# A hybrid encoder step on one core: sums for the feed-forward made beside the output projections, and norm roots with tokens on partitions

## The chip, the cores and the metric

The kernel runs on one core of a Trainium2 chip. The core has five engines that run side by side, each through its own list of instructions in order: TensorE (PE, matmuls; PEld is its load of weights), VectorE (DVE), ScalarE (ACT), GpSimd (POOL) and SyncE (SP, which issues transfers). They wait for each other through semaphores. The metric is the device time of one execution, in microseconds, as the median of several runs.

## What is computed

One inference step of a two-layer encoder over 1072 tokens (32 of a sample, 16 meta tokens and 1024 of a prompt), 1024 features, in fp32. Every layer is

```python
x += mixer(rms_norm(x)) @ w_out          # layer 0: gated delta rule and S5; layer 1: two kinds of attention
h = rms_norm(x)
x += (silu(h @ w1) * (h @ w3)) @ w2      # feed-forward, 2816 wide
```

and a last `rms_norm` follows, with `rms_norm(x) = x * rsqrt(mean(x*x) + 1e-6) * gain`. The states and caches that the mixers leave are outputs too.

## The kernel before

Features lie on partitions and tokens on columns, so x is eight tiles `X[0..7]` of 128 features by 1072 tokens. The columns are cut in three chunks (360, 360, 352). To keep fp32 accuracy, every operand is split in a high part (ACT, L37 or L40) and a low part (DVE, L38 or L41), and each product is three matmuls (`mm3`, L72 to L74).

**The feed-forward** multiplies by w1 and w3 with a scheme of seven products for each 2 by 2 block (`quad`, Strassen-Winograd). The columns are halved (HN = 536) and the features too, so that `X[i]` and `X[i + 4]` form a pair, i = 0..3, with the blocks B11 and B12 (first and second half of the columns of `X[i]`) and B21 and B22 (of `X[i + 4]`). Seven right operands come from them: B11, B21, B22, and the sums T1 to T4, each for four pairs: 28 units, each a tile with its high and low part. T1 is the second half less the first of `X[i]`; T2, T3 and T4 need both tiles of a pair (`s_early`, L170 to L173, three scalar-tensor-tensors on DVE with the gain multiplied in). `s_late` makes the other sixteen, with the subtractions of T1 on POOL (L188). The weights have sums of their own, S1 to S4, on POOL (L206 to L209). The products run in the order B11, T2, B21, T3, T1, T4, B22, each as 24 matmuls of 268 columns (`pq`, L225); the first leaves its PSUM bank by ACT (L230). Eleven steps of `ffn` each take two row blocks of w1 and w3. The result goes through DRAM to the product with w2.

**The seam** is what lies between a layer's output projection and these products. The units are tiles of pools that `open_ffn` opens: 16 slots `mv`, 3 `ot`, 9 `us`, and scratch `sab`. It is called when the projections' own tiles (the mixers' output split in high and low part: `lh`, `ll`, `rh`, `rl` in layer 0, `mxh`, `mxl` in layer 1) are given back, so that no unit has a place before.

In layer 0, `out_part` adds the projection tile by tile to X (L1248): m = 5, 6, 7 with all twelve mixes, then 0 to 4 with the last eight. In layer 1 the loop over `ORD` (5, 6, 7, 0 to 4) adds the product of the heads 0 to 6 (L1473); the share of the eighth, `m7`, follows in a pass of 72 matmuls over all tiles (L1487).

**The norm** is not applied ahead of the products: its root `r` is multiplied into their results. `sq_acc` sums the squares of X over the tiles (ACT L94, POOL L95); `norm_r` sums over the partitions with a matmul by a matrix of ones (L83), so that every partition has the sum of each column, and takes Sqrt (L84) and the reciprocal (L85) of 128 by 360 values.

The order on each engine is set by a scheduler that weighs each instruction by estimated times; a tile that a pool reuses makes its first writer wait for the last reader of what lay there.

Of the kernel before, what the change touches and what calls it, by code (L numbers as in the profile page):

```python
# [11 lines left out]
T = 1072  # L12
# [3 lines left out]
SQ = 448  # L16
# [60 lines left out]
def norm_r(cx, acc, r, c0, c1, n=D, ps=None):  # L77

    nc = cx.nc
    p = (cx.ps.tile([128, 512], F32, name="pm", bufs=cx.npm) if ps is None else ps)[:, :c1 - c0]  # L80
    accs = acc if isinstance(acc, list) else [acc]
    for i, a in enumerate(accs):
        nc.tensor.matmul(p, cx.ones, a[:, c0:c1], start=i == 0, stop=i == len(accs) - 1)  # L83
    nc.scalar.activation(r[:, c0:c1], p, AF.Sqrt, bias=cx.eps, scale=1.0 / n)  # L84
    nc.vector.reciprocal(r[:, c0:c1], r[:, c0:c1])  # L85


def sq_acc(cx, x, acc, k, c0, c1, eng=None):
# [4 lines left out]
    s = cx.tp.tile([128, SQ], F32, name="sq", bufs=2)[:, :c1 - c0]  # L93
# [27 lines left out]
def open_ffn(cx, m7=None):  # L121

    cx.fA, cx.fB = ExitStack(), ExitStack()
    pa = cx.fA.enter_context(tpool(cx.tc, "fa"))
    pb = cx.fB.enter_context(tpool(cx.tc, "fb"))
    cx.tp = cx.fB.enter_context(tpool(cx.tc, "ftmp", 2))
    n = [0, 0]

    def slot(nm, bufs, dt=F32):
        return pa.tile([128, T], dt, name=nm, bufs=bufs)  # L130

    def us():
# [30 lines left out]
def s_early(cx, B, gain, i):  # L163
# [8 lines left out]
    v.scalar_tensor_tensor(b[:, n1], x1[:, n0], g1, b[:, n0], op0=OP.mult, op1=OP.add)  # L172
    v.scalar_tensor_tensor(a[:, n1], x2[:, n0], g2, b[:, n1], op0=OP.mult, op1=OP.subtract)  # L173
    for nm, src in (("T2", b[:, n1]), ("T3", b[:, n0]), ("T4", a[:, n1])):
        B[nm][i] = cx.us()
        s_parts(cx, src, B[nm][i])


def s_late(cx, B, gain):
    nc = cx.nc  # L180
    n0, n1 = slice(0, HN), slice(HN, T)
    for nm, h, n in (("B11", 0, n0), ("B21", 4, n0), ("T1", 0, None), ("B22", 4, n1)):
        for i in PAIRS:
            B[nm][i] = cx.slot("mv", 16, F32R)
            x, g = cx.X[i + h], gain[:, i + h:i + h + 1]
            if n is None:
                d = cx.sab()[:, n0]
                nc.gpsimd.tensor_sub(d, x[:, n1], x[:, n0])  # L188
                s_parts(cx, d, B[nm][i], scale=g)
            else:  # L190
                s_parts(cx, x[:, n], B[nm][i], scale=g)
# [6 lines left out]
def quad(cx, raws, B, first):  # L198
# [7 lines left out]
    g.tensor_add(S1, A21, A22)  # L206
    g.tensor_sub(S2, S1, A11)
    g.tensor_sub(S3, A11, A21)
    g.tensor_sub(S4, A12, S2)  # L209
# [38 lines left out]
def ffn(cx, w1, w3, w2, B, chunks, done, out=None):  # L248
# [3 lines left out]
    r = cx.slot("r", 1)  # L252
# [7 lines left out]
    with tpool(cx.tc, "sps", space=PSUM) as cx.ps:  # L260
        for t in range(0, 22, 2):
# [12 lines left out]
            o1, o2 = quad(cx, wa, B, gate)  # L274
# [5 lines left out]
            u1, u2 = quad(cx, wb, B, lambda o, p: v.tensor_mul(two(o), p, two(o1[:, :HN])))  # L280
# [70 lines left out]
def setup2(cx, tc, ctx, I):  # L351
# [395 lines left out]
def even_layer(cx, ctx, I, O):  # L747
# [13 lines left out]
    with ExitStack() as es:  # L761
# [1287 lines left out]
```

## Time and profile before

| | |
|---|---|
| median of 3 runs | 3412.39 us (3411.39 to 3413.61) |
| the profiled execution | 3411.61 us, of which the span is 3409.8 |
| PE busy | 3169.7 us, 93% |
| DVE, ACT, POOL busy | 58%, 35%, 32% |
| mean granted clock of PE | 0.964 |

The span is the stretch from the first to the last instruction of the trace. Busy times are sums over the whole span, while the seams are short; so they are read from stretches and from the rows of one engine in time. In such a row the first number is the start, the second the duration (of all, where a count stands behind), and brackets give the idle time of the engine ahead of it and what ended it.

### The profile page before, as it was taken

What the parts mean: (1) busy time and instruction counts of PE and PEld (TensorE: products, weight loads), DVE (VectorE), ACT (ScalarE), POOL (GpSimd) and SP (SyncE); (2) the same over time, 40 slices, a digit from 0 to 9 for tenths busy, and PEclk for the clock granted to TensorE, in tenths of its full rate; (3) what the DMA queues carried; (4) which work ended last, traced back from release to release, by engine and by line L of the source; (5) the groups of instructions that cost most, each with busy time, mean ns of one, the idle gap of its engine ahead of it and who ended that gap; (6) DMA issues with size and microseconds to landing.
All of it is one profiled execution on the core that took longest, in us unless ns stands there. A gap on an engine that the chain in (4) does not pass through costs nothing.

```text
span 3409.8 us, 54300 instructions
## 1 busy us (share of the span) xinstructions
PE 3169.7 (93%) x21511; PEld 3028.3 (89%) x21511; DVE 1961.1 (58%) x3590; ACT 1198.4 (35%) x2201; POOL 1092.5 (32%) x1080
## 2 busy tenths in 40 slices
PE   7998999999996999999999999998897899999997
PEld 6998998888895999999999998876687899999996
DVE  8666448945426555556338226657767655556435
ACT  5543222145523222223114115555653322223112
POOL 2144564512223555541003002223213655551003
PEclk9999999999998999999999999998898899999998
DMA  2355323356431222226123445544333222226212
GB/s 102 129 172 162 112 84 111 93 178 258 162 119 57 77 82 76 76 83 221 55 58 124 156 139 139 157 140 118 91 124 117 69 76 76 82 76 222 76 41 70
DMA packets 159525, 388.53 MB, mean 114 GB/s; under 512 B 40908, under 2 KB 72032, under 8 KB 159272
## 3 DMA queue, kind: packets, MB, share of 16 engines
q1 hardware_dynamic: 135096, 317.84, 29.8%
q10 hardware_dynamic: 16704, 44.33, 3.5%
q0 software_dynamic: 7472, 22.91, 2.0%
q8 instruction: 169, 2.77, 0.3%
q14 instruction: 84, 0.69, 0.1%
HBM read 265.44 MB, written 119.56 MB: 113 GB/s over the span
## 4 chain that ended last, share of the span: by engine, by line
PE 66%; DVE 5%; DMA 3%; ACT 2%; issue 2%; POOL 1%; SPq 0%; ACTq 0%; DVEq 0%; POOLq 0%
PE pq L225 26%; PE pm L72 10%; PE pm L73 10%; PE pm L74 10%; PE po L1765 1%; PE S L1583 1%; PE S L1580 1%; DVE mv L41 1%; PE tr L1760 1%; PE po L1847 1%; DMA sab<-ud 0%; PE pm L1695 0%; DMA rraw<-mixd 0%; POOL aQ L1568 0%; ACT P L1792 0%
## 5 line engine op out<-in xcount | busy, mean ns | idle before, releaser
L72 PE MATMUL pm<-mv,wh 128*128 128x360 f32 (+2 forms) x2080 | 692.2, 333 | 23.6 <-DVE pre L914 12.5
L73 PE MATMUL pm<-mv,wh 128*128 128x360 f32 (+2 forms) x2080 | 687.9, 331 | 0.0
L74 PE MATMUL pm<-mv,wl 128*128 128x360 f32 (+2 forms) x2080 | 685.4, 330 | 0.0
L72 PEld LDWEIGHTS pm<-mv,wh 128*128 128x128 f32 (+1 forms) x2080 | 393.5, 189 | 35.0 <-issue 12.8
L73 PEld LDWEIGHTS pm<-mv,wh 128*128 128x128 f32 (+1 forms) x2080 | 393.3, 189 | 4.4 <-issue 1.3
L37 ACT ACTIVATE wh<-wraw 128x1024 fp32r<-128x1024 f32 (+6 forms) x180 | 148.4, 824 | 706.5 <-PE pm L73 607.9
L74 PEld LDWEIGHTS pm<-mv,wl 128*128 128x128 f32 (+1 forms) x2080 | 393.5, 189 | 3.1 <-issue 0.2
L225 PE MATMUL pq<-mv,wl 128*128 128x268 f32 x2112 | 290.1, 293 | 36.4 <-ACT xslot L230 27.2
L225 PEld LDWEIGHTS pq<-mv,wl 128*128 128x128 f32 x2112 | 278.0, 195 | 39.9 <-ACT xslot L230 28.8
L95 POOL TENSOR_TENSOR acc<-acc,sq 128x360 f32<-128x360 f32 (+3 forms) x77 | 84.6, 1106 | 668.9 <-ACT sq L94 668.2
L225 PE MATMUL pq<-mv,wh 128*128 128x268 f32 x2112 | 279.1, 286 | 2.0 <-ACT wh L37 1.4
L225 PEld LDWEIGHTS pq<-mv,wh 128*128 128x128 f32 x2112 | 267.8, 188 | 2.6 <-ACT wh L37 1.9
L225 PE MATMUL pq<-us,wh 128*128 128x268 f32 x1188 | 163.6, 288 | 15.4 <-ACT wh L37 14.2
L312 DVE TENSOR_TENSOR xslot<-xslot,pm 128x360 f32<-128x360 f32 x144 | 75.2, 526 | 175.5 <-PE pm L74 175.4
L225 PEld LDWEIGHTS pq<-us,wh 128*128 128x128 f32 x1188 | 154.2, 190 | 16.3 <-ACT wh L37 16.3
L38 DVE TENSOR_TENSOR wl<-wraw,wh 128x1024 fp32r<-128x1024 f32 (+6 forms) x142 | 134.6, 948 | 53.1 <-ACT wh L37 51.6
L225 PE MATMUL pq<-us,wl 128*128 128x268 f32 x1188 | 162.3, 288 | 0.0
L225 PEld LDWEIGHTS pq<-us,wl 128*128 128x128 f32 x1188 | 153.6, 190 | 0.0
L279 POOL TENSOR_TENSOR xslot<-xslot,r 128x1072 f32<-128x1072 f32 x44 | 122.4, 2804 | 0.2
L921 DVE SCALAR_TENSOR_TENSOR cy<-pre,convw,cy 128x1104 f32<-128x1104 f32 x72 | 112.1, 1557 | 13.6 <-ACT cy L919 12.1
L38 DVE TENSOR_TENSOR wh<-sab,wh 128x512 fp32r<-128x512 f32 x88 | 78.7, 896 | 64.9 <-ACT wh L37 64.9
L1580 PE MATMUL S<-aKh,aQ 128*128 128x512 f32 (+9 forms) x240 | 91.8, 384 | 18.7 <-DVE mxs L1791 6.9
(718 smaller groups left out, 7152.8 us busy)
## 6 DMA issues: line engine op xcount, KB each, us to landing
ud<-xslot SPq DMA_DIRECT2D x44, 536.0 KB
sab<-ud SPq DMA_DIRECT2D x44, 536.0 KB
wraw<-in_w_dram SPq DMA_DIRECT2D x44, 512.0 KB
xraw<-in_w_dram SPq DMA_DIRECT2D x44, 512.0 KB
wraw<-in_wie_dram SPq DMA_DIRECT2D x36, 512.0 KB
qkvd<-cy ACTq DMA_DIRECT2D x24, 552.0 KB
wraw<-in_wio_dram SPq DMA_DIRECT2D x24, 512.0 KB
kq<-qkvd SPq DMA_DIRECT2D x16, 552.0 KB
```

The lines of the kernel that those rows point to most:

```text
L37: nc.scalar.activation(h, src, AF.Copy)
L38: (eng or nc.vector).tensor_sub(l, src, f(h))
L41: nc.vector.scalar_tensor_tensor(l, src, scale, f(h), op0=OP.mult, op1=OP.subtract)
L72: nc.tensor.matmul(ps, a, h[:, c0:c1], start=start and k == 0, stop=False)
L73: nc.tensor.matmul(ps, a, l[:, c0:c1], start=False, stop=False)
L74: nc.tensor.matmul(ps, b, h[:, c0:c1], start=False, stop=stop and k == kt - 1)
L95: (eng or nc.gpsimd).tensor_add(acc[:, c0:c1], acc[:, c0:c1], s)
L225: nc.tensor.matmul(p[:, 512 * j:512 * j + HC], op[:, wo + 128 * k:wo + 128 * k + 128], B[nm][k][:, xo + HC * j:xo + HC * j + HC], start=ne ...
L279: g.tensor_mul(o, o, r)
L312: nc.vector.tensor_add(X[m][:, c0:c1], X[m][:, c0:c1], p)
L921: v.scalar_tensor_tensor(y[:, :TG], pre[:, j:j + TG], convw[:, i, j:j + 1], y[:, :TG], op0=OP.mult, op1=OP.add)
L1580: nc.tensor.matmul(pt, lhs, Kh[:, k0:k0 + n], start=True, stop=False)
```

## The change

Five things change.

- **Pools.** `open_fa` (slots `mv`, `ot`, `r`) is opened ahead of the last part of the output projection. In layer 0 the late mixes now lie in `mv` slots themselves, with `ot` as landing place. `open_fb` (`us`, `sab`) follows, and a table `UNITS` says for every unit which kind of slot it takes, and in which order. In layer 0 the units of pairs 1 and 2 take `us`, which lies over `rh` and `rl`, and most others `mv`. In layer 1 they lie over the first four mixes, and in the tiles of `m7` and of the mixes 4 to 6 (`u7`, `u8`).
- **Order of tiles.** In layer 0 `m = 5` and `6` are projected together, first with the old mixes, then with the late ones. In layer 1 the order is 5, 6, 7, 1, 2, 3, 0, 4, and `m7` is the eighth head of the loop; the pass behind it is gone.
- **Engines.** The additions of squares beside the projections, the subtractions of T1, and S1 to S4 of the first step (`t == 0`) go from POOL to DVE.
- **Order of sums.** `s_all` makes T2 to T4 of pairs 1 and 2, B11, then pairs 3 and 0, then B21, T1 and B22. `s_early` splits T2 as soon as it is there.
- **Norm.** `norm_r` multiplies the slices of 128 tokens by one column of ones, so that the sums have tokens on partitions. Sqrt and reciprocal work on up to three columns; a second matmul per slice, by the identity, spreads them over the partitions again, and ACT copies the result to `r`. This holds for the norms at the start of both layers and at the end, too.

```diff
 def norm_r(cx, acc, r, c0, c1, n=D, ps=None):
-    for i, a in enumerate(accs):
-        nc.tensor.matmul(p, cx.ones, a[:, c0:c1], start=i == 0, stop=i == len(accs) - 1)
-    nc.scalar.activation(r[:, c0:c1], p, AF.Sqrt, bias=cx.eps, scale=1.0 / n)
-    nc.vector.reciprocal(r[:, c0:c1], r[:, c0:c1])
+    cuts = [(i, c, min(c + 128, c1)) for i, c in enumerate(range(c0, c1, 128))]
+    q = p[:, 508:512]
+    for i, a, b in cuts:
+        for j, x in enumerate(accs):
+            nc.tensor.matmul(q[:b - a, i:i + 1], x[:, a:b], cx.ones[:, 0:1], start=j == 0, stop=j == len(accs) - 1)
+    s = r[:, c0:c0 + 4]
+    for x0, x1, m in ((0, len(cuts) - 1, 128), (len(cuts) - 1, len(cuts), cuts[-1][2] - cuts[-1][1])):
+        nc.scalar.activation(s[:m, x0:x1], q[:m, x0:x1], AF.Sqrt, bias=cx.eps[:m], scale=1.0 / n)
+        nc.vector.reciprocal(s[:m, x0:x1], s[:m, x0:x1])
+    for i, a, b in cuts:
+        nc.tensor.matmul(p[:, a - c0:b - c0], s[:b - a, i:i + 1].to_broadcast([b - a, 128]), cx.ident[:b - a, :b - a], start=True, stop=True)
+    nc.scalar.activation(r[:, c0:c1], p[:, :c1 - c0], AF.Copy)
...
+UNITS = (
+    [("us", n, i) for i in (1, 2) for n in ("T2", "T3", "T4")] + [("us", "B11", i) for i in (1, 2, 3)] +
+    [("ot", "B11", 0), ("ot", "T2", 3), ("ot", "T3", 3), ("mv", "T4", 3)] + [("mv", n, 0) for n in ("T2", "T3", "T4")] +
+    [("mv", n, i) for n in ("B21", "T1", "B22") for i in PAIRS],
...
+def s_block(cx, B, gain, nm):
...
-                nc.gpsimd.tensor_sub(d, x[:, n1], x[:, n0])
+            cx.nc.vector.tensor_sub(d, x[:, n1], x[:, n0])
...
+def s_all(cx, B, gain):
+    s_early(cx, B, gain, 1)
+    s_early(cx, B, gain, 2)
+    s_block(cx, B, gain, "B11")
+    s_early(cx, B, gain, 3)
+    s_early(cx, B, gain, 0)
+    for nm in ("B21", "T1", "B22"):
+        s_block(cx, B, gain, nm)
...
-            o1, o2 = quad(cx, wa, B, gate)
+            o1, o2 = quad(cx, wa, B, gate, g if t else v)
...
+    with esX:
+        open_fa(cx)
         open_psum(cx, False)
-        mv += [load_mix(k, sp, "l", 7) for k in range(1, 8)]
-        out_part(range(5, 8), [(mvs, 0), (mv, 4)], cx.pmt, True)
-        out_part(range(5), [(mv, 4)], cx.pmt, True)
+        mv = [load_mix(k, ltiles) for k in range(8)]
+        out_part([5, 6], [(mvs, 0), (mv, 4)], cx.pmt, True)
+        out_part([7], [(mvs, 0), (mv, 4)], cx.pmt, True)
+        for m in range(5):
+            out_part([m], [(mv, 4)], cx.pmt, True)
...
-ORD = list(range(NF, 8)) + list(range(NF))
+ORD = [5, 6, 7, 1, 2, 3, 0, 4]
...
-        mix += [parts(k, mp) for k in range(4, 7)]
+        mix += [parts(k, lambda n: more["u8"]()) for k in range(4, 7)] + [m7]
...
-                mm3(cx, p, w, mix[k0:], 7 - k0, 128, c0, c1)
+                mm3(cx, p, w, mix[k0:], 8 - k0, 128, c0, c1)
                 v.tensor_add(x[:, c0:c1], x[:, c0:c1], p)
+                sq_acc(cx, x, cx.acc, i, c0, c1, v)
```

How the change moves instructions shows in the order on the engines. First DVE in layer 0, around the last evictions of the projection (L1248 before, L1279 after); `xslot` and `xraw` are tiles of X. Before, the evictions stand alone and all sums follow:

```order
L1248 TENSOR_TENSOR xslot<-xslot,pm 128x360 x2
L1248 TENSOR_TENSOR xslot<-xslot,pm 128x352
L38 TENSOR_TENSOR wl<-wraw,wl 128x512
L1248 TENSOR_TENSOR xslot<-xslot,pm 128x360 x2
L1248 TENSOR_TENSOR xslot<-xslot,pm 128x352
L41 SCALAR_TENSOR_TENSOR mv<-xraw,gain,mv 128x536
L41 SCALAR_TENSOR_TENSOR mv<-xslot,gain,mv 128x536 x3
```

After, in the same place, with the sums of pair 3 (L192 to L195) and their splits among the evictions of the last tile:

```order
L192 SCALAR_TENSOR_TENSOR sab<-xslot,gain,sab 128x536
L193 SCALAR_TENSOR_TENSOR sab<-xslot,gain,sab 128x536
L195 SCALAR_TENSOR_TENSOR sab<-xslot,gain,sab 128x536
L1279 TENSOR_TENSOR xslot<-xslot,pm 128x360
L38 TENSOR_TENSOR ot<-sab,ot 128x536 x2
L104 TENSOR_TENSOR acc<-acc,sq 128x360
L1279 TENSOR_TENSOR xslot<-xslot,pm 128x360
L38 TENSOR_TENSOR mv<-sab,mv 128x536
L104 TENSOR_TENSOR acc<-acc,sq 128x360
L1279 TENSOR_TENSOR xslot<-xslot,pm 128x352
L192 SCALAR_TENSOR_TENSOR sab<-xslot,gain,sab 128x536
L208 TENSOR_TENSOR sab<-xraw 128x536
```

Three of four pairs, and B11, have moved ahead of the last eviction; pair 0, T1 (L208), B21 and B22 still follow it.

Next PE at the start of layer 1's feed-forward. Before, the end of the pass for `m7` (its tiles are called `sab`), B11, the norm, B21 and the first matmuls of T2:

```order
L74 MATMUL pm<-sab,wl 128x352
L225 MATMUL pq<-mv,wl 128x268 x24
L83 MATMUL pm<-acc,ones 128x360 x2
L83 MATMUL pm<-acc,ones 128x352
L225 MATMUL pq<-mv,wl 128x268 x24
L225 MATMUL pq<-us,wh 128x268 x4
```

After, where the last projection matmul is one of the loop:

```order
L74 MATMUL tr<-u_22125,wl 128x352
L255 MATMUL pq<-mv,wl 128x268 x24
L87 MATMUL pm<-ones,acc 128x1 x2
L87 MATMUL pm<-ones,acc 104x1
L87 MATMUL pm<-ones,acc 128x1 x2
L87 MATMUL pm<-ones,acc 104x1
L93 MATMUL pm<-ident,r 128x128 x2
L93 MATMUL pm<-ident,r 128x104
L93 MATMUL pm<-ident,r 128x128 x2
L93 MATMUL pm<-ident,r 128x104
L255 MATMUL pq<-mv,wl 128x268 x2
```

Each norm has become two visits to PE, one column per slice (L87) and a spreading matmul (L93), which here stand directly behind each other, between B11 and B21.

## Rows read from the trace of the kernel before

**Rows 1.** The page: busy us of each engine, share of the span, instructions
```profile
PE 3169.7 (93%) x21511; PEld 3028.3 (89%) x21511; DVE 1961.1 (58%) x3590; ACT 1198.4 (35%) x2201; POOL 1092.5 (32%) x1080
```

**Rows 2.** What PE waited for: us in all, times, longest
```profile
PE pq L225 <- ACT xslot L230: 27.2, 2, 24.5
...
PE pm L83 <- POOL acc L95: 19.4, 3, 11.3
```

**Rows 3.** Layer 0's seam: length, busy us of PE, PEld, DVE, ACT, POOL, granted clock
```profile
1040.00:1060.00 20.00, 19.90 (x120) 19.35 (x119) 3.48 (x8) 4.05 (x8) 4.79 (x5) 1.00 0.11 41
1060.00:1080.00 20.00, 4.94 (x28) 3.38 (x27) 20.00 (x24) 12.05 (x21) 1.59 (x1) 0.79 0.07 28
1080.00:1105.00 25.00, 7.50 (x35) 6.97 (x36) 22.32 (x24) 12.62 (x20) 17.86 (x10) 0.57 0.20 63
1105.00:1150.00 45.00, 43.38 (x334) 42.99 (x334) 28.63 (x30) 13.12 (x19) 24.57 (x15) 0.95 0.21 72
```

**Rows 4.** PE there, in time: start, us, instruction, count, idle before with releaser
```profile
1058.73 0.32 PE L74 MATMUL pm<-lh,wl 128*128 128x352 f32 x1
...
1062.76 2.97 PE L225 MATMUL pq<-mv,wl 128*128 128x268 f32 x22 [0.47 <-DVE mv L41]
...
1092.26 4.63 PE L225 MATMUL pq<-mv,wl 128*128 128x268 f32 x24 [24.51 <-ACT xslot L230]
...
1104.29 4.83 PE L225 MATMUL pq<-mv,wl 128*128 128x268 f32 x20 [1.83 <-DVE wl L38]
```

**Rows 5.** DVE in the same stretch
```profile
1059.09 0.52 DVE L1248 TENSOR_TENSOR xslot<-xslot,pm 128x352 f32<-128x352 f32 x1 [3.34 <-PE pm L74]
...
1060.56 2.15 DVE L41 SCALAR_TENSOR_TENSOR mv<-xslot,gain,mv 128x536 fp32r<-128x536 f32 x3
...
1065.97 4.66 DVE L85 RECIPROCAL r<-r 128x360 f32<-128x360 f32 x2
...
1078.63 1.97 DVE L38 TENSOR_TENSOR us<-sab,us 128x536 fp32r<-128x536 f32 x3
...
1098.39 4.17 DVE L41 SCALAR_TENSOR_TENSOR mv<-xslot,gain,mv 128x536 fp32r<-128x536 f32 x3
```

**Rows 6.** POOL in the same stretch
```profile
1094.40 1.79 POOL L206 TENSOR_TENSOR sab<-wraw 128x512 f32<-128x512 f32 x1
```

**Rows 7.** Stretches of layer 1's seam, columns as in rows 3
```profile
2580.00:2600.00 20.00, 20.00 (x125) 20.00 (x124) 9.93 (x18) 2.64 (x4) 0.00 (x0) 1.00 0.26 77
2620.00:2640.00 20.00, 6.25 (x16) 3.08 (x15) 19.96 (x21) 11.34 (x22) 12.18 (x10) 0.59 0.00 0
2640.00:2665.00 25.00, 10.08 (x42) 9.46 (x43) 25.00 (x22) 10.36 (x17) 15.16 (x10) 0.57 0.21 64
```

**Rows 8.** PE in layer 1's seam, columns as in rows 4
```profile
2612.20 0.32 PE L74 MATMUL pm<-sab,wl 128*128 128x352 f32 x1
...
2662.80 3.72 PE L225 MATMUL pq<-mv,wl 128*128 128x268 f32 x15 [1.45 <-DVE wl L38]
```

**Rows 9.** DVE there: additions that read PSUM
```profile
2601.92 2.27 DVE L1487 TENSOR_TENSOR xraw<-xraw,pm 128x360 f32<-128x360 f32 x5
```

**Rows 10.** PE in time: the first matmul with a late mix
```profile
957.97 0.65 PE L72 MATMUL pm<-lh,wh 128*128 128x360 f32 x3
```

**Rows 11.** ACT in time: the last two splits of late mixes
```profile
968.01 1.10 ACT L37 ACTIVATE lh<-lraw 128x1072 fp32r<-128x1072 f32 x1 [1.30 <-DMA lraw<-mixd]
972.45 1.10 ACT L37 ACTIVATE lh<-lraw 128x1072 fp32r<-128x1072 f32 x1 [3.33 <-DMA lraw<-mixd]
```

**Rows 12.** A stretch of layer 0's start, columns as in rows 3
```profile
30.00:40.00 10.00, 7.73 (x35) 5.77 (x34) 10.00 (x23) 4.90 (x6) 3.11 (x4) 0.86 0.01 2
```

**Rows 13.** DVE in time at the end
```profile
3383.33 2.45 DVE L85 RECIPROCAL mv<-mv 128x368 f32<-128x368 f32 x1 [6.47 <-ACT mv L84]
...
3395.63 1.75 DVE L85 RECIPROCAL mv<-mv 128x256 f32<-128x256 f32 x1 [1.82 <-ACT mv L84]
```

**Rows 14.** PE in time at the end
```profile
3393.86 1.22 PE L83 MATMUL pm<-acc,ones 128*128 128x256 f32 x2 [3.43 <-DVE acc L95]
```

More of the change, by code (lines that the diff above doesn't have):

```diff
@@ L92, in sq_acc @@
         return
-    s = cx.tp.tile([128, SQ], F32, name="sq", bufs=2)[:, :c1 - c0]
+    s = cx.sqt()[:, :c1 - c0]
     nc.scalar.activation(s, x[:, c0:c1], AF.Square)
@@ L172, in s_early, with quad @@
     v.scalar_tensor_tensor(b[:, n1], x1[:, n0], g1, b[:, n0], op0=OP.mult, op1=OP.add)
+    s_parts(cx, b[:, n1], B["T2"][i])
     v.scalar_tensor_tensor(a[:, n1], x2[:, n0], g2, b[:, n1], op0=OP.mult, op1=OP.subtract)
[L174 to L180, printed above, removed]
-    n0, n1 = slice(0, HN), slice(HN, T)
[L182 to L187, printed above, removed]
-                nc.gpsimd.tensor_sub(d, x[:, n1], x[:, n0])
-                s_parts(cx, d, B[nm][i], scale=g)
-            else:
-                s_parts(cx, x[:, n], B[nm][i], scale=g)
+    s_parts(cx, b[:, n0], B["T3"][i])
+    s_parts(cx, a[:, n1], B["T4"][i])
+def s_block(cx, B, gain, nm):
+    n0, n1 = slice(0, HN), slice(HN, T)
+    h, n = {"B11": (0, n0), "B21": (4, n0), "T1": (0, None), "B22": (4, n1)}[nm]
+    for i in PAIRS:
+        x, g = cx.X[i + h], gain[:, i + h:i + h + 1]
+        if n is None:
+            d = cx.sab()[:, n0]
+            cx.nc.vector.tensor_sub(d, x[:, n1], x[:, n0])
+            s_parts(cx, d, B[nm][i], scale=g)
+        else:
+            s_parts(cx, x[:, n], B[nm][i], scale=g)
+def s_all(cx, B, gain):
[6 more added lines that the diff above has]
+        s_block(cx, B, gain, nm)
 def two(ap):
     return ap.rearrange("p (b n) -> p b n", b=2)
-def quad(cx, raws, B, first):
+def quad(cx, raws, B, first, eng):
     nc = cx.nc
@@ L1427, in odd_layer @@
     m7 = esM.enter_context(tpool(tc, "m7"))
-    m7p, m7 = m7, [m7.tile([128, T], F32R, name="sab", bufs=2) for e in range(2)]
+    m7p, m7 = m7, [m7.tile([128, T], F32R, name="u7", bufs=2) for e in range(2)]
     def out_w(m, k0, k1):
@@ L1437, in odd_layer, with parts @@
             at.diff(m7, 3)
-        def parts(k, pool):
+        def parts(k, slots):
             raw = hi.tile([128, T], F32, name="oraw", bufs=2)
@@ L1446, in parts @@
                 g.tensor_mul(raw[:, 32:], raw[:, 32:], w)
-            h, l = (pool.tile([128, T], F32R, name=n, bufs=4) for n in ("mxh", "mxl"))
+            h, l = (slots(n) for n in "hl")
             split(cx, raw, h, l)
             return h, l
-        mix = [parts(k, hi) for k in range(4)]
+        mix = [parts(k, lambda n: hi.tile([128, T], F32R, name="mx" + n, bufs=4)) for k in range(4)]
         for m in range(NF):
@@ L1459, in odd_layer @@
             g.dma_start(xd2[m], x)
+        m8 = esM.enter_context(tpool(tc, "m8"))
         cx.open_x(None)
         cx.X = cx.new_x()
-        mp = es.enter_context(tpool(tc, "mx2"))
-        mix += [parts(k, mp) for k in range(4, 7)]
+        more = {n: (lambda p=p, n=n, b=b: p.tile([128, T], F32R, name=n, bufs=b)) for p, n, b in ((m7p, "u7", 2), (m8, "u8", 6))}
+        mix += [parts(k, lambda n: more["u8"]()) for k in range(4, 7)] + [m7]
         for i, m in enumerate(ORD):
@@ L1990, in program @@
         even_layer(cx, ctx, I, O)
-        open_ffn(cx)
-        B = new_units()
-        for i in PAIRS:
-            s_early(cx, B, cx.gain[:, 2], i)
-        s_late(cx, B, cx.gain[:, 2])
+        B = open_fb(cx, 0, {})
+        s_all(cx, B, cx.gain[:, 2])
         mov = []
```

110 lines of the change are left out of this document (51 added, 59 removed).

## The prediction

> **What bounds the kernel now.** I read the page first. PE is busy for 93% of the span and DVE for 58% [rows 1]. So the kernel is bound by TensorE almost everywhere, and a gain can only come from the few places where PE waits. The list of waits names them: 24.5 us in one piece for ACT's copy of a product's bank, and 11.3 us for POOL's additions to the sum of squares [rows 2]. The stretches and the engines' own rows place them in the two seams, between the last output projection of a layer and its feed-forward. In layer 0 PE is full until 1060, then busy 4.94 of 20 us and 7.50 of 25, and nearly full again from 1105 [rows 3]. In the two empty stretches DVE is busy 20.00 of 20 and 22.32 of 25: the vector engine is the bound of the seam, because all 28 units are made there. Just ahead of the seam it is busy 3.48 of 20 us. Layer 1 looks alike: DVE has half its time free at 2580, and is full from 2620 to 2665, with PE at 6.25 of 20 and 10.08 of 25 [rows 7].
>
> My yardstick for a seam is the time from the end of the last projection matmul to the main part of the product T1, the last that waits for the sums; from there PE is nearly full. In layer 0 that is 1104.29 - (1058.73 + 0.32) = 45.2 us [rows 4]; in layer 1 it is 2662.80 - (2612.20 + 0.32) = 50.3 us [rows 8].
>
> **Prices.** On DVE a 536-column scalar-tensor-tensor takes 2.15 / 3 = 0.70 us while POOL is idle and 4.17 / 3 = 1.39 beside POOL; a plain 536-column one takes 1.97 / 3 = 0.66 [rows 5]. An addition of 360 columns that reads PSUM takes 2.27 / 5 = 0.45 [rows 9]; I take the same for a square's addition. The new reciprocals are of three columns or fewer; no row shows one, so I bound them by 0 and 1.75, the shortest shown, and take 0.1, since the long ones go with their columns: 1.75 us for 256, 2.45 for 368 [rows 13].
>
> **Layer 0's seam.** Where three of the four pairs used to wait for the pool, their sums now stand between the evictions of the projections, on a DVE with 16.5 of 20 us free [rows 3]; I cost those at nothing. Behind the last eviction the order leaves, up to the split of S1 that T1 needs: 3 + 12 scalar-tensor-tensors (15 x 0.70 = 10.5), 12 plain ones (5 splits, the 4 subtractions of T1, S1 to S3: 12 x 0.66 = 7.9), one square's addition (0.45) and six small reciprocals (0.6). That is 19.5 us, with the last eviction of 0.52 20.0. The first four reciprocals wait for a PE that does B11 first (some 3 us), then a Sqrt on ACT: I add 1 us, an estimate. So T1 starts at 21 instead of 45.2: **-24 us**. Behind it little changes: S4 and the splits of S2 and S3 follow on DVE while PE does T1, as now. PE itself needs B11, B21 and the small matmuls before T1, 2.97 to 4.63 us for a product [rows 4], and is not late. What goes from POOL to DVE (four subtractions, eight S) is in this count for the part that T1 waits for; the second quad's four S come later (2.6 us), beside PE's products, where DVE was busy 28.63 of 45.
>
> Bounds: at 1.39 us for all 27 operations the list is 18 to 20 us longer, and only some 5 us of gain are left. I take the uncontended price, since in the new order POOL has nothing between the last mixer's work and the S of the next pair of weights. The other end is T1's own operands without the rest of the list, some 17 us: -28.
>
> The mix loads are the cover to watch. All eight mixes now come late; the first 72 matmuls (m = 5 and 6 on the old heads) cover 72 x 0.166 = 12 us [rows 3], as long as the first late mix took now: PE reached it at 957.97, 12 us into the stretch [rows 10]. After that each mix is 18 matmuls, 3 us, so the eighth is wanted at about 979. The last two splits now start at 968.01 and 972.45 [rows 11], so one load more is some 4.4 us, and a split on ACT and DVE 2.4 (an estimate: 1.10, and 1.3 after it): ready at about 979. I charge **+1** (0 to 4).
>
> **Layer 1's seam.** The 72 matmuls of the last head stay 72, only inside the loop: nothing gained there, and the end of the projections stays. In the last four tiles of the loop PE has 144 matmuls of 20.00 / 125 = 0.16 [rows 7], 23.0 us, and DVE, by the order, 12 evictions and 8 square additions (9.0), 13 scalar-tensor-tensors (9.1) and 10 plain ones (6.6): 24.7. It falls 1.7 us behind. Behind the last eviction stand 15 x 0.70, 14 x 0.66, 4 x 0.45 and six small ones: 22.1, with the eviction 22.7; with the arrears T1 starts at about 24.4 instead of 50.3: **-26** (-6 if all were contended, -30 at best).
>
> **The norm roots elsewhere.** A norm now crosses PE twice more. In the odd layer's start PE is full and 23 matmuls stand between the two visits: 0. At layer 0's start DVE is full and PE loses 2.27 of 10 us [rows 12]; with the long reciprocals gone: **-2** (-2.3 to +2). At the end two reciprocals stand alone on the way, 2.45 and 1.75 us [rows 13], against two more crossings of PE and a copy on ACT. The ones-matmul of the last takes 1.22 [rows 14]; I take **-3** (-6 to +1). The loads of w2's operands wait for differently ordered slots: 0 +- 2 each.
>
> **Sum.** -24 + 1 - 26 - 2 - 3 = -54. Against its own run, 3411.6 us (span 3409.8 and 1.8 around it), that is 3357.6; the median stands 0.8 above it: **3358 us**.
>
> [...]
>
> **Rivals.** *POOL still slows DVE.* Its next S (four at 1.79 us [rows 6]) need only weights and a free tile, and may start inside the new seam: 7 us at half speed are 3.5 us a seam; were the whole list slowed, the seams give 5 and 6 us. Between these: 3366 to 3394, say 3376. For it: every contended row. Against: the order. [...]
>
> *The early sums don't run early*, because the tiles they take are freed only at the end. Then all units still follow the last eviction, some 34 us uncontended instead of 45 and 50: 3383.
>
> *Slower: the norm's second visit blocks PE.* PE takes its instructions in order, so a spreading matmul whose reciprocal is queued behind DVE's sums stops all behind it. There are 15 such visits; from 54 / 15 = 3.6 us each they eat the whole gain, and at 4.5 us the time is 3411.6 - 54 + 67 = 3425. For: in the seam the reciprocals stand behind eight DVE instructions. Against: 23 matmuls stand between in the odd layer and at the end, and in the seams PE would idle anyway.
>
> *More gain:* both seams and the end at their best bounds, -28, -30, -2, -6 and a clock that comes back sooner: about 3342.
>
> **Chances.** Forecast 0.68 (3345 to 3370), POOL 0.15, sums late 0.05, slower 0.05, more gain 0.07. The range 3342 to 3388 takes in the forecast, most of the POOL case and its neighbour. A measurement can tell about 0.2% here, 7 us. Faster 0.92, same 0.03 (a mixture of part losses), slower 0.05.
>
> **What would show it.** Right: scalar-tensor-tensors of 536 columns between the evictions at 1040, at 0.70 us; T1's main part some 21 and 24 us after the last projection; a hole of PE of 6 to 9 us in each seam; no long reciprocal. Wrong: DVE rows of 1.4 us in the seam; holes of PE at 958 to 979 or inside the projections; a spreading matmul with more than 2 us of idle time ahead of it outside the seams.

## The result, and the profile after

The changed kernel takes 3358.97 us in the median (3356.13 to 3361.62) against 3411.89 us before: a ratio of 0.9844, 95% interval 0.9827 to 0.9861. The prediction was 3358. The profiled execution has a span of 3358.3 us, 51.5 less than before.

The busy times on the page answer to [rows 1]. PE has hardly changed, POOL has lost 86 us of work, and what is gone is waiting:

```profile
PE 3180.8 (95%) x21673; PEld 3046.4 (91%) x21673; DVE 1924.1 (57%) x3646; ACT 1199.3 (36%) x2228; POOL 1006.0 (30%) x1014
```

Layer 0's seam in stretches, with the columns of [rows 3]:

```profile
1040.00:1060.00 20.00, 18.16 (x126) 17.92 (x125) 15.93 (x30) 11.24 (x23) 0.00 (x0) 1.00 0.23 82
1060.00:1080.00 20.00, 14.70 (x85) 14.03 (x86) 18.61 (x31) 10.59 (x20) 0.00 (x0) 0.74 0.18 53
1080.00:1105.00 25.00, 24.23 (x196) 24.02 (x195) 15.25 (x16) 8.83 (x12) 17.26 (x10) 1.00 0.20 64
```

In the first of these stretches, of which the last 8 us are already seam here, DVE does 15.93 of 20 us instead of 3.48; in the 20 us up to the end of the last projection matmul it is 14.85 instead of 3.33. PE has one poor stretch instead of two, and POOL does nothing until the seam is over. PE's rows there answer to [rows 4]:

```profile
1051.47 0.32 PE L74 MATMUL pm<-mv,wl 128*128 128x352 f32 x1
...
1052.37 2.38 PE L255 MATMUL pq<-us,wl 128*128 128x268 f32 x18
1054.59 1.31 PE L87 MATMUL pm<-ones,acc 128*128 128x1 f32 x12
1056.37 1.55 PE L93 MATMUL pm<-ident,r 128*128 128x128 f32 x12 [0.46 <-ACT r L90]
...
1063.17 4.71 PE L255 MATMUL pq<-mv,wl 128*128 128x268 f32 x22 [1.44 <-DVE mv L41]
...
1070.57 1.26 PE L255 MATMUL pq<-mv,wh 128*128 128x268 f32 x4 [2.05 <-ACT wh L37]
1071.63 4.13 PE L255 MATMUL pq<-mv,wl 128*128 128x268 f32 x24
```

T1's main part starts 1071.63 - (1051.47 + 0.32) = 19.8 us after the last projection matmul, instead of 45.2. DVE's rows, which answer to [rows 5], show no price of 1.39 us any more:

```profile
1041.82 0.78 DVE L192 SCALAR_TENSOR_TENSOR sab<-xslot,gain,sab 128x536 f32<-128x536 f32 x1
...
1056.06 0.49 DVE L91 RECIPROCAL r<-r 128x2 f32<-128x2 f32 x4
...
1060.97 2.15 DVE L41 SCALAR_TENSOR_TENSOR mv<-xslot,gain,mv 128x536 fp32r<-128x536 f32 x3
```

Sums now run among the evictions, three scalar-tensor-tensors take 2.15 us together, and four small reciprocals 0.49, where two long ones took 4.66.

Layer 1's seam, on PE, answers to [rows 8]:

```profile
2582.95 0.33 PE L74 MATMUL tr<-u,wl 128*128 128x352 f32 x1
...
2592.82 1.58 PE L93 MATMUL pm<-ident,r 128*128 128x128 f32 x6 [1.24 <-ACT r L90]
...
2600.76 5.28 PE L255 MATMUL pq<-mv,wl 128*128 128x268 f32 x22 [1.99 <-DVE mv L41]
...
2607.69 2.70 PE L255 MATMUL pq<-u,wl 128*128 128x268 f32 x20
```

2607.69 - 2583.28 = 24.4 us, instead of 50.3. 

Where the 51.5 us lie, by the same points in both traces (the first matmul by the identity ahead of layer 0's output projection, end of the last projection matmul, T1's main part, first matmul of w2, end):

| stretch | before | after | difference | predicted |
|---|---|---|---|---|
| start to the output projection of layer 0 | 943.6 | 936.6 | -7.0 | -2 |
| output projection of layer 0 | 115.5 | 115.2 | -0.3 | +1 |
| seam of layer 0 | 45.2 | 19.8 | -25.4 | -24 |
| T1 to w2, layer 0 | 459.0 | 455.5 | -3.5 | 0 |
| w2 of layer 0 to the last projection of layer 1 | 1049.2 | 1056.2 | +7.0 | 0 |
| seam of layer 1 | 50.3 | 24.4 | -25.9 | -26 |
| T1 to w2, layer 1 | 458.0 | 460.5 | +2.5 | 0 |
| w2 of layer 1 to the end | 289.0 | 290.1 | +1.1 | -3 |

The seams came as worked out. The terms around them did not: the start gave 5 more, the stage of layer 1's mixer took 7, and these cancel. This is one execution of each kernel; a second profile of the changed one, further down, has the seams within 0.5 us of these, but the start 3.3 us longer, and the stage of layer 1's mixer as much.

### The profile page after: what moved, and what is told of

Read it like the earlier page. It is cut to its first block, busy times and chain, and to the rows that moved or that the text cites. A ratio compares the mean times of both kernels' runs of the same rounds, so it can differ in the third digit from the quotient of the medians.

```text
span 3358.3 us, 54622 instructions
## 1 busy us (share of the span) xinstructions
PE 3180.8 (95%) x21673; PEld 3046.4 (91%) x21673; DVE 1924.1 (57%) x3646; ACT 1199.3 (36%) x2228; POOL 1006.0 (30%) x1014
## 5 line engine op out<-in xcount | busy, mean ns | idle before, releaser
L72 PE MATMUL pm<-mv,wh 128*128 128x352 f32 (+2 forms) x2272 | 749.5, 331 | 21.7 <-DVE pre L940 9.0
L74 PE MATMUL pm<-mv,wl 128*128 128x352 f32 (+2 forms) x2272 | 746.2, 329 | 0.9 <-DVE wl L38 0.9
L73 PE MATMUL pm<-mv,wh 128*128 128x352 f32 (+2 forms) x2272 | 746.8, 329 | 0.0
L72 PEld LDWEIGHTS pm<-mv,wh 128*128 128x128 f32 (+1 forms) x2272 | 427.8, 188 | 33.0 <-issue 8.6
L73 PEld LDWEIGHTS pm<-mv,wh 128*128 128x128 f32 (+1 forms) x2272 | 427.7, 188 | 4.5 <-issue 1.1
L37 ACT ACTIVATE wh<-wraw 128x1024 fp32r<-128x1024 f32 (+4 forms) x179 | 148.2, 828 | 673.9 <-PE pm L73 570.1
L104 POOL TENSOR_TENSOR acc<-acc,sq 128x360 f32<-128x360 f32 (+3 forms) x35 | 35.4, 1012 | 512.8 <-ACT sq L103 512.2
L38 DVE TENSOR_TENSOR wl<-wraw,wh 128x512 fp32r<-128x512 f32 (+4 forms) x141 | 133.9, 949 | 47.9 <-ACT wh L37 46.3
L255 PE MATMUL pq<-us,wl 128*128 128x268 f32 x858 | 119.2, 287 | 0.0
L255 PE MATMUL pq<-us,wh 128*128 128x268 f32 x858 | 118.6, 286 | 0.0
L255 PEld LDWEIGHTS pq<-us,wl 128*128 128x128 f32 x858 | 111.6, 189 | 0.0
L255 PEld LDWEIGHTS pq<-us,wh 128*128 128x128 f32 x858 | 111.0, 188 | 0.0
```

The source lines that it names most:

```text
L37: nc.scalar.activation(h, src, AF.Copy)
L38: (eng or nc.vector).tensor_sub(l, src, f(h))
L72: nc.tensor.matmul(ps, a, h[:, c0:c1], start=start and k == 0, stop=False)
L73: nc.tensor.matmul(ps, a, l[:, c0:c1], start=False, stop=False)
L74: nc.tensor.matmul(ps, b, h[:, c0:c1], start=False, stop=stop and k == kt - 1)
L104: (eng or nc.gpsimd).tensor_add(acc[:, c0:c1], acc[:, c0:c1], s)
```

## The experiments

Ratios are to the kernel before, on the same chip. The runs come from several chips, and the kernel before takes 3408.03 to 3411.89 us on them; so kernels from different chips are compared by their ratios. All seams are measured as above, in the one profiled execution of each kernel.

### The old norm root in all places

The changed kernel with the `norm_r` of before.

```diff
-    cuts = [(i, c, min(c + 128, c1)) for i, c in enumerate(range(c0, c1, 128))]
...
+    nc.vector.reciprocal(r[:, c0:c1], r[:, c0:c1])
```

> The changed kernel with the norm roots as before (a matmul by a matrix of ones, Sqrt and reciprocal of 128 by 360); all else as changed. Theory (DVE's list bounds the seam): three reciprocals of 2.3 us come back into each seam's list in place of six of 0.1, so T1's main part starts 6 to 7 us later in each seam, 26 and 31 us after the last projection instead of 19.8 and 24.4; layer 0's start loses 2 to 7 us again: 3374 to 3379 us. Rival (the roots' new form gives nothing, its two visits to PE cost what the reciprocals save): T1 within 2 us of where it is, and the 7 us that the attention stage lost with the change come back: 3350 to 3360 us.

Measured: 3372.25 us, 0.9889 (0.9874 to 0.9904). The seams are 26.8 us (+6.9) and 31.0 (+6.6), as the theory had it, layer 0's projection ends 6.4 us later, w2 to the end takes 289.7 instead of 290.1. In layer 1's seam DVE is late with B21, and ACT with a split of the weights; PE's rows in this kernel:

```profile
2610.28 4.90 PE L246 MATMUL pq<-mv,wl 128*128 128x268 f32 x22 [6.62 <-DVE mv L41]
2618.44 1.26 PE L246 MATMUL pq<-mv,wh 128*128 128x268 f32 x4 [3.26 <-ACT wh L37]
```

So the small reciprocals are worth some 7 us in each seam and 6 at the start, and nothing at the end. The stage of layer 1's mixer took 1046.8 us here, 9 less than with the new root; that became the open question below.

Layer 0's start shows where most of the 6 us come from. The changed kernel, then this one, columns as in [rows 3]:

```profile
30.00:40.00 10.00, 10.00 (x74) 9.29 (x72) 9.09 (x41) 6.22 (x13) 3.58 (x4) 1.00 0.01 2
```

```profile
30.00:40.00 10.00, 7.78 (x36) 5.92 (x35) 10.00 (x21) 5.24 (x7) 3.44 (x4) 0.88 0.01 2
```

The stretch 30 to 40, on which the prediction rested, gave its 2.2 us; in it PE waited for the sums of the norm itself. The rest is spread: over the first 250 us PE waits 7.5 us instead of 10.5 for the products of a projection with the root, which DVE makes behind the reciprocals.

### The sums held back

The changed kernel, with the gain made to depend on the last eviction, so that no sum starts earlier.

```diff
 def s_all(cx, B, gain):
+    cx.nc.vector.scalar_tensor_tensor(gain, cx.X[4][:, T - 8:T], 0.0, gain, op0=OP.mult, op1=OP.add)
```

> The changed kernel, but in both layers the gain that scales the sums is made to depend on the last eviction of the projections by one small instruction, so that no unit can be made beside the projections; slots, engines, norm and merged head stay. Theory (the early sums are the larger part of the gain): the list behind the last eviction grows from 27 and 33 to all 28 units, 28 scalar-tensor-tensors and 21 plain ones, some 35 us at uncontended prices, so T1's main part starts at 35 to 37 us instead of 19.8 and 24.4: 3385 to 3389 us. Rival (the relief from POOL and the shorter reciprocals gave it, the early slots little): T1 at most 5 us later in each seam, 3360 to 3369 us.

Measured: 3385.68 us, 0.9929 (0.9913 to 0.9946). The seams are 35.2 us (+15.4) and 34.0 (+9.6), in layer 1 a microsecond under the theory's range. The sums that stand between the evictions are the largest single part of the two seams' gain, and the larger half of layer 0's.

### Subtractions and the first S back on POOL

```diff
-            cx.nc.vector.tensor_sub(d, x[:, n1], x[:, n0])
+            cx.nc.gpsimd.tensor_sub(d, x[:, n1], x[:, n0])
...
-            o1, o2 = quad(cx, wa, B, gate, g if t else v)
+            o1, o2 = quad(cx, wa, B, gate, g)
```

> The changed kernel with the four subtractions of T1 and S1 to S4 of the first step on POOL again, in the early slots. Theory (POOL slows DVE to half beside it, so that moving work to POOL doesn't relieve DVE): seven instructions of 0.65 us leave DVE's list ahead of T1, 4.6 us, but the seven POOL instructions of some 1.75 us, 12 us, slow DVE beside them by half, which is 6 us and more; and T1 waits for POOL's chain: T1 2 to 6 us later in each seam, 3363 to 3371 us. Rival (two engines share the list): T1 4 us earlier in each seam, 3349 to 3353 us.

Measured: 3360.33 us, 0.9851 (0.9835 to 0.9868), within the uncertainty of the changed kernel's. The seams are longer, 21.9 us (+2.1) and 32.4 (+8.0): T1 comes later, as the theory has it, in layer 1 by more than its 2 to 6 us. But most of layer 1's is given back: PE does 24 matmuls of T2 ahead of T1's main part there, T1 to w2 took 455.6 us instead of 460.5, and 3.1 are left at w2. The start was 2.3 us shorter, which is within what two executions of one kernel differ by. So the time lies between the theory's 3363 to 3371 and the rival's 3349 to 3353. DVE beside POOL in layer 1's seam, then POOL:

```profile
2601.47 4.16 DVE L41 SCALAR_TENSOR_TENSOR mv<-xslot,gain,mv 128x536 fp32r<-128x536 f32 x3
...
2606.93 2.14 DVE L41 SCALAR_TENSOR_TENSOR u<-xslot,gain,u 128x536 fp32r<-128x536 f32 x3
```

```profile
2600.93 1.75 POOL L237 TENSOR_TENSOR sab<-sab,wraw 128x512 f32<-128x512 f32 x1
2602.75 1.62 POOL L239 TENSOR_TENSOR sab<-wraw,sab 128x512 f32<-128x512 f32 x1
```

Three instructions of one form take 4.16 us beside POOL and 2.14 alone. That is the price of the rival "POOL still slows DVE", 1.39 and 0.71 each; its condition didn't arise in the changed kernel, whose POOL works again only after the seam.

### B22's units behind the rest

The last four units that stand ahead of S1's split on DVE are made behind it.

```diff
-    for nm in ("B21", "T1", "B22"):
+    for nm in ("B21", "T1"):
         s_block(cx, B, gain, nm)
+    def late(o):
+        cx.nc.vector.scalar_tensor_tensor(gain, o[:, :8], 0.0, gain, op0=OP.mult, op1=OP.add)
+        s_block(cx, B, gain, "B22")
...
     first(o1[:, :HN], product(A12, "B21", "A"))
+    if cx.late:
+        cx.late(o1)
```

> The changed kernel with the units of B22 (four scalar-tensor-tensors of 0.70 us in each seam's list) made only after B21's product has been multiplied by the root, so behind the split of S1, by a small instruction that makes their gain depend on it; the last product alone uses them. Theory (DVE's list, counted one by one, sets T1's start): T1's main part 2.8 us earlier in each seam, at 17 and 21.6 us after the last projection, with B22 still in time: 3353 to 3355 us. Rival (PE's own chain of B11, norm and B21 is as late as the list): T1 moves by less than 1 us: 3358 to 3360 us.

Measured: 3352.39 us, 0.9831 (0.9817 to 0.9846). Layer 0's seam is 17.9 us (-2.0), nearer to the theory; layer 1's is 24.1, the rival's: there PE comes to T1 late itself, since B21's 22 matmuls take 5.28 us there, as in the changed kernel, where the granted clock was 0.50 during them. The profiled execution is 7.2 us shorter than the changed kernel's, more than the seams explain; 4.8 of it is the stage of layer 1's mixer, 1051.4 us. The two ratios differ by 0.0013, some 4 us, and their intervals overlap.

### Two parts alone in the kernel before

First the eighth head in the loop, and nothing else:

```diff
-        w = out_w(m, k0, 7)
+        w = out_w(m, k0, 8)
...
-                mm3(cx, p, (wh[:, m], wl[:, m]), [m7], 1, 128, c0, c1)
```

> The kernel before, with one part of the change alone: the eighth head is a part of the loop over the tiles, and the pass of 72 matmuls behind it is gone; sums, engines, pools and norm are as before. Theory (the prediction's: PE's work is the same, nothing is gained): the seam of layer 1 stays at 49 to 51 us from the last projection matmul to the main part of T1, and the time is within 4 us of the kernel before. Rival: the pass behind the loop cost the vector engine 24 additions of 0.45 us in the stretch where the sums begin, 10.9 us; with them gone the sums begin earlier relative to the last matmul, the seam is 40 to 46 us, and the time is 5 to 11 us less than before.

Measured: 3407.16 us, 0.9995 (0.9986 to 1.0004); the seam of layer 1 is 48.2 us, 2.1 less, between the two ranges expected. "Nothing gained there" is right within what can be measured. Then the new root, and nothing else:

```diff
-    nc.vector.reciprocal(r[:, c0:c1], r[:, c0:c1])
+    cuts = [(i, c, min(c + 128, c1)) for i, c in enumerate(range(c0, c1, 128))]
...
```

> The kernel before with the new norm root alone. Theory: in each seam three reciprocals of 2.33 us stand on DVE ahead of the operands of T1, so each seam gives 6 to 7 us, and layer 0's start gives the 6 that it gave in the changed kernel: 18 to 21 us less than before, 3388 to 3392 on this chip's scale of 3408. Rival: the seam of before is held by the sums and POOL's additions, and the root waits for those anyway; only layer 0's start gains, 5 to 8 us less than before.

Measured: 3403.06 us, 0.9986 (0.9972 to 0.9999). The seams are 40.6 us (-4.6) and 45.9 (-4.3), and layer 0's projection ends 6.3 us earlier: 15 us, somewhat less than the theory. Yet only 7 are left in the time, which is the rival's total, though the seams are not the rival's. In the profile the stage of layer 1's mixer took 1061.8 us, 12.6 more than before; but the profiled execution, 3412.44 us, is 9.4 above the median of this kernel's ten, so part of that belongs to the execution.

### Where layer 1's mixer loses time

By now the stage from w2 to the last projection of layer 1 took 1046.8 to 1051.9 us in the three kernels with the old root at its start, and 1051.4 to 1061.8 in the five with the new one. Its first part, up to the end of a hole of PE at the start of the second attention, took 729.4 to 735.6 us with the old root and 727.6 to 735.1 with the new: no loss there. In the changed kernel, PE and then DVE, which ends the hole:

```profile
2254.93 0.47 PE L1601 MATMUL S<-aKh,aQ 128*128 128x128 f32 x1 [5.67 <-DVE mxs L1812]
```

```profile
2252.16 2.25 DVE L1555 CAST mkb<-lo 128x256 bf16<-128x256 f32 x1 [6.18 <-DMA lo<-in_amask_dram]
2254.33 0.55 DVE L1812 CUSTOM_DVE_ANT_0 P<-S,bias 128x384 f32<-128x384 f32 x1
```

DVE stands in a cast that waits for the load of the second attention's mask, and the row maxima of the first stand behind it. In the kernel before, the same place on PE reads

```profile
2294.57 0.47 PE L1580 MATMUL S<-aKh,aQ 128*128 128x128 f32 x1 [3.25 <-DVE mxs L1791]
```

So my theory was that the load's late landing costs the time. I made two kernels: the old root at the start of layer 1 alone, and the mask kept from the first attention.

```diff
-                    norm_r(cx, cx.acc, r, c0, c1, ps=cx.pmt())
+                    norm_o(cx, cx.acc, r, c0, c1, ps=cx.pmt())
```

> The changed kernel, with the old norm root at the start of layer 1 alone. The stage from w2 of layer 0 to the end of layer 1's projections took 1056.2 us in the changed kernel and 1049.2 before. Rival: the new norm's two visits to PE disturb that stage; with the old one it takes 1046 to 1050, and the time is 3349 to 3353. Theory: the loss lies 550 us later, where the second attention waits for its mask (a hole of 5.7 us on PE instead of 3.3, and the clock at 0.67 for the 72 us behind it instead of 0.80); the norm is not concerned, the stage takes 1051 to 1058 by when the mask lands, and the time is 3354 to 3361.

Measured: 3350.48 us, 0.9828 (0.9808 to 0.9849), the stage 1043.2 us, in a profiled execution of 3344.42 us, the fastest of four. The time is the rival's, and my theory falls: the hole is there (6.19 us), and the stage is short all the same.

```diff
+        if hasattr(self.cx, "mkb"):
+            self.identb, self.mkb = self.cx.identb, self.cx.mkb
+            return
```

> The changed kernel, with the mask of the first attention kept for the second, which loads and casts none. Theory: the hole of PE ahead of the second attention's fourth score tile (5.67 us in the changed kernel, released by DVE, which stood in a cast that waited for the mask's load) shrinks to under 1 us, the clock of the 72 us behind it rises from 0.67 to 0.80 or more, the stage from w2 of layer 0 to the end of layer 1's projections takes 1046 to 1050 us instead of 1056, and the time is 6 to 10 us less than the changed kernel's. Rival: the clock falls there because the products of the attention wait for ACT and DVE anyway; only the hole goes, 3 to 4 us, or nothing.

Measured: 3350.29 us, 0.9824 (0.9802 to 0.9847), the stage 1048.5 us in an execution 5.2 us above the median, as this theory had it; but not by its mechanism. The hole has grown. PE and DVE in this kernel:

```profile
2259.74 0.48 PE L1604 MATMUL S<-aKh,aQ 128*128 128x128 f32 x1 [6.83 <-DVE mxs L1815]
```

```profile
2258.60 0.23 DVE L1830 TENSOR_TENSOR dl<-dl 128x64 f32<-128x64 f32 x1 [7.09 <-DMA dl<-in_dlam_dram]
```

With the mask gone DVE waits in the same place for the next load of POOL's queue. So the hole does not decide; it also changes from one execution of a kernel to another, 5.67 and 3.57 us in the two profiles of the changed kernel, 6.19 and 3.36 with the old root at layer 1's start. The loss lies behind it. From the end of the hole to the last projection matmul every kernel has 1762 to 1765 matmuls on PE in the trace; they took

| kernel | us | PE busy | clock |
|---|---|---|---|
| before | 318.0 | 287.7 | 0.92 |
| merged head alone | 316.3 | 286.7 | 0.92 |
| old root in all places | 317.4 | 288.6 | 0.91 |
| old root at layer 1's start | 316.8 | 285.8 | 0.93 |
| the same, second profile | 323.6 | 291.6 | 0.91 |
| mask kept | 318.4 | 289.3 | 0.91 |
| changed | 328.4 | 298.5 | 0.89 |
| changed, second profile | 330.2 | 295.1 | 0.90 |
| B22 late | 323.8 | 290.3 | 0.91 |
| POOL | 327.1 | 292.4 | 0.91 |
| sums held | 329.2 | 296.2 | 0.89 |
| norm alone | 326.7 | 296.2 | 0.89 |

The second profiles are those of the runs below. Two rows of it, the changed kernel and the one with the old root at layer 1's start, each from the end of its hole on (columns as in [rows 3]):

```profile
2254.93:2583.28 328.35, 298.53 (x1764) 252.85 (x1764) 219.87 (x606) 190.16 (x428) 59.50 (x73) 0.89 0.38 117
```

```profile
2250.92:2567.73 316.81, 285.81 (x1764) 243.43 (x1764) 220.88 (x606) 190.84 (x428) 59.11 (x73) 0.93 0.40 121
```

The same matmuls keep PE busy 12.7 us longer, which is more than the whole difference of 11.5: the engine waits some 30 us in both, but its mean granted clock is 0.89 instead of 0.93. The other rows don't all go by the clock alone: with POOL, PE is busy 292.4 us and waits 34.7. One piece of the same work, at its first and its last row, in the changed kernel and in the other:

```profile
2284.95 1.70 PE L1781 MATMUL tr<-ident,P 128*128 128x128 f32 x6
...
2292.51 0.59 PE L1786 MATMUL po<-PTl,VS 128*128 128x272 f32 x1
```

```profile
2277.62 1.09 PE L1794 MATMUL tr<-ident,P 128*128 128x128 f32 x6
...
2282.17 0.39 PE L1799 MATMUL po<-PTl,VS 128*128 128x272 f32 x1
```

The same 28 matmuls take 7.56 us at a granted clock of 0.50 and 4.55 at 1.00, and PE has no idle time in either. In the first ten microseconds behind its hole the clock is 0.50 to 0.60 in all twelve profiles; over the first 40 it is 0.63 and 0.59 in the two of the changed kernel, and 0.67 to 0.76 in the others.

Is that chance, or does it belong to a kernel? Four kernels ran beside each other: the changed one again,

> The changed kernel itself, unchanged, as the yardstick for the three that go beside it, and as a second profile of it. If the 1056.2 us of the stage from w2 of layer 0 to the end of layer 1's projections belong to this order of instructions, the stage takes 1053 to 1059 again and the time is 3356 to 3362; if it is chance of single executions (in which the clock falls for longer or shorter behind the hole of the second attention), the stage is as likely at 1046 to 1052 and the times of the runs spread over 8 us or more.

which took 3362.49 us (3360.24 to 3366.77), 0.986 (0.9839 to 0.988), with the stage at 1059.4 us and the seams at 19.4 and 24.4: both lie just above the first range, and the loss is there again. That speaks for the kernel, though two executions are few. Then the one with the old root at layer 1's start again,

> The changed kernel with the old norm root at the start of layer 1, a second time, now beside the changed kernel itself. Theory (the new norm there costs time, by another order of DVE's instructions in the second attention): 6 to 10 us less than the changed kernel, with the stage from w2 of layer 0 to the end of layer 1's projections at 1043 to 1050. Rival (chance of executions): the medians of the two kernels are within 3 us.

which took 3356.08 us (3351.81 to 3360.51), 0.9839 (0.9818 to 0.9861), 6.4 us less than the changed kernel, with the stage at 1053.3 us. The theory of this pair holds at its lower edge in time and misses in the stage: 1043 and 1053 are two executions of one kernel, so a good half of what the first showed was chance. Then all loads between the attentions made early, lambda's too:

```diff
-        dl = self.t([128, 4, 64], "dl", 1)
-        g.dma_start(dl, I['dlam'].to_broadcast([128, 256]).rearrange("p (a b) -> p a b", a=4))
...
+        dg, lam = cx.dg, cx.lam
```

> The changed kernel, with the mask kept from the first attention and the two small vectors of the second (gain and lambda) loaded, and lambda worked out, at the start of the first, so that DVE waits for no load between the two attentions. In the run with the mask kept alone DVE waited at that place for the next load of the same queue instead, 7.09 us, and PE 6.83. Theory: the hole of PE there shrinks to under 2 us, the clock of the 40 us behind it rises from 0.5 to 0.7 to above 0.85, and the time is 4 to 10 us less than the changed kernel's on this chip. Rival: PE waits there for the loads and splits of the next head's maps (ACT and POOL) anyway; the hole stays at 3 us or more, the clock falls as before, and the time is within 3 us of the changed kernel's.

It took 3356.95 us (3354.33 to 3360.92), 0.9844 (0.9823 to 0.9864), with the stage at 1053.8 us. DVE waits for no load there any more, and PE's hole has become one for ACT, a little later:

```profile
2266.44 0.59 PE L1803 MATMUL po<-PTh,VS 128*128 128x272 f32 x1 [4.51 <-ACT PTh L37]
```

The time is 5.5 us less than the changed kernel's, as the theory had it, but the hole and the clock are the rival's: behind it the clock is 0.53 for ten microseconds. Neither explains both. Last, three edits together:

> All that helped together: B22's units behind T1's, the old norm root at the start of layer 1, and the early loads between the attentions. If the gains add up (6.6, some 8, and what the early loads bring, 0 to 8): 3336 to 3346 against some 3359 of the changed kernel. If the gains of the last two are the same stage's chance, 3348 to 3353, as with B22 late alone.

It took 3356.27 us (3352.39 to 3360.93), 0.984 (0.9819 to 0.9862): the gains do not add up, as the second expectation said, though not at its time. Layer 0's seam with what follows it, up to w2, took 472.0 us as with B22 late alone, instead of 475.3 and 473.7 in the two profiles of the changed kernel, and the stage took 1054.9.

One thing goes along with the lengths in part: the order that the scheduler gave to DVE's instructions of the second attention, some 440. In the kernel before and the two runs that went with it in the stage (old root in all places, merged head) it is the same, and their stages took 1046.8 to 1051.9 us. "B22 late", "POOL", "norm alone", "loads early" and "combined" share another but for one place; the changed kernel's is some 30 places away from that, and all six are 150 to 190 places away from the first. Their stages took 1051.4 to 1061.8 us. "Combined" is among these although its root at layer 1's start is the old one. "Old root at layer 1's start", "mask kept" and "sums held" each have an order of their own, more than 50 places away from every other, and took 1043.2 and 1053.3, 1048.5, and 1057.9 us. So the root is not the cause by itself. That the order is, through the places where PE waits and its clock falls, is not shown: one kernel's two executions stand 10 us apart, as far as the groups do, and no run changed the order alone. It stays open.

## Why the prediction was right

- **The bound.** Right: DVE's list behind the last eviction set both seams, in layer 1 together with B21 on PE. Holding the sums back gave 15.4 and 9.6 us of the 25.4 and 25.9 away again, the old root 6.9 and 6.6, POOL 2.1 and 8.0; the merged head had given 2.1 of layer 1's. Counted from the last projection matmul to w2, where the order of T1 and T2 on PE makes no difference, they are 15.8, 8.2 and 2.5 of 29.0 us in layer 0 and 8.2, 9.0, 3.1 and 2.5 of 23.4 in layer 1. The parts come near the whole, though each was taken alone.
- **The signs named.** Scalar-tensor-tensors stand between the evictions at 1040, at 0.78 us one by one and 0.72 in a row; PE is idle for 6.2 us of the one seam and 7.1 of the other, where a hole of 6 to 9 was named, though in several pieces of 2.3 us at most; no norm has a long reciprocal any more.
- **Layer 0's seam, 21 us forecast, 19.8 measured.** The prices of 0.70 and 0.66 us were those of the rows, and the list had the right length. The microsecond added for the first roots was not needed: PE did B11 and the sums over the partitions while DVE went on, and DVE has no idle time of note up to T1. Its list ended 19.3 us behind the start of the last eviction, where 20.0 were counted.
- **Layer 1's seam, 24.4 forecast, 24.4 measured.** The arrears were right: DVE began the last eviction 1.9 us after the last projection matmul, where it was to fall behind by 1.7. But the list with the split of S1 ended after 23.5 us, and B22's experiment says that it was not DVE's list alone: with four units fewer in it T1 came only 0.3 us earlier, because B21 on PE, 22 matmuls in 5.28 us in both kernels, at a granted clock of 0.50 in the changed one, ended as late. That the sum came out exactly is partly luck.
- **The clock in the seam.** The rival *more gain* lets it come back sooner; what that is worth no run shows by itself. B21, behind PE's idle time, ran slow in both seams: 22 matmuls in 4.71 us in layer 0 and 5.28 in layer 1, at granted clocks of 0.59 and 0.50, where 18 of B11 ahead took 2.38 in layer 0 at 1.00. T1 started slow in layer 0 (24 matmuls in 4.13 us, granted clock 0.73), but not in layer 1 (20 in 2.70, at 1.00), nor in layer 0 of the second profile, where 24 took 3.12:

```profile
1072.99 3.12 PE L255 MATMUL pq<-mv,wl 128*128 128x268 f32 x24
```

- **POOL.** As the order had it, POOL's first instruction comes at 1083.42 in layer 0, behind the seam. The price of the rival was right, as the run with POOL shows: 1.39 us instead of 0.71. Three instructions beside two of POOL's, of 1.75 and 1.62 us, took 2.0 us longer in all than three alone.
- **The mix loads**, +1 forecast, -0.3 measured: PE waited 0.47 us for a split of one of them, and 0.38 for one of the weights.
- **The merged head**, 0 forecast: right to 0.05% in the time, though the seam alone became 2.1 us shorter.
- **The start, -2 forecast, -7.0 measured.** Mis-sized: the step took the one stretch [rows 12] as the whole of it. Over the first 250 us PE waits 3.1 us less for DVE's products with the root and no longer the 2.3 for the sums of the norm. In the second profile the start gave only 3.7.
- **The odd layer, 0 forecast, +7.0 measured.** Mis-sized: the step looked at the norm's own place, and there is indeed no wait. The loss lies some 730 us later, in a part that the change does not touch: behind the hole PE is busy 298.5 us instead of 287.7, at a clock of 0.89 instead of 0.92, and waits no longer than before. Why is open.
- **The end, -3 forecast, +1.1 measured.** The two long reciprocals are gone, but with the old root the changed kernel's end takes 289.7 us instead of 290.1: nothing was won. The first of the norms there waits for POOL's sum of squares, in the changed kernel too (PE's row):

```profile
3328.26 1.38 PE L87 MATMUL pm<-ones,acc 128*128 128x1 f32 x6 [5.78 <-POOL acc L104]
```

- **Two of the rivals' times** were added up wrongly, by 2 to 3 us: seams that give 5 and 6 us come to 3397, not 3394, and seams of 34 us to 3381, not 3383. Neither changes a chance. The run with the sums held back, at 35.2 and 34.0, took 3385.68.

Forecast and measurement differ by -5.0 (start), -1.3 (mixes), -1.4 and +0.1 (seams), +7.0 (mixer of layer 1), +4.1 (end), -3.5 and +2.5 (T1 to w2, taken as 0 ± 2): +2.5 in all, 51.5 us instead of 54. The two seams were worked out from rows and came so; the other terms were off by 1 to 7 us each, and that they cancelled is luck.

## What to carry over

Where one engine makes the operands of the next stage, count its list behind the last result it needs, at the price of each form that a row shows, and move into the idle places ahead what needs only part of that result: that gave 15 of 25 us in layer 0's seam and 10 of 26 in layer 1's. A long instruction on a full engine can cost more than the wait seen beside it: at the start a wait of 2.2 us was seen, and 6 us came back. And a stage that a change does not touch can differ by as much as the change gains in one of its small parts, here 7 to 10 us; compare the stages by their ends, and by more than one execution, before believing a total.

## What the runs showed of the hardware

- The reciprocal goes with its columns: 4.66 us for two of 360 columns [rows 5], 0.49 us for four of 2 columns and fewer. The roots of two chunks cost PE 1.31 us for the matmuls of one column and 1.55 us for the spreading ones, twelve of each in the trace.
- The length of layer 1's mixer behind the hole hung on the clock as much as on waits: the same 1762 to 1765 matmuls kept PE busy 285.8 us at a mean granted clock of 0.93, up to 298.5 at 0.89, and its waits between them were 28.8 to 35.1 us in all.
- The same small load took four times as long where the DMA engines were full. The mask, loaded through POOL's queue for both attentions of the changed kernel, landed 2.3 us after its issue at 1992.68, with the DMA engines' busy share at 0.27 in those 2.3 us, and 9.5 us after its issue at 2242.59, with the share at 1. DVE's cast of it starts at 2252.16, with nothing else in its way. With the mask kept, the load that stood in its place, issued at 2249.18, landed after 9.4 us.
